# A decoder block's residual gate: summed on TensorE, or along rows on VectorE

## The chip, the cores and the metric

One NeuronCore of a Trainium2 chip runs one program. The metric is the device time of one execution in microseconds (us), the median of several runs. The engines are TensorE (PE, with its weight loads PEld), VectorE (DVE), ScalarE (ACT), GpSimd (POOL) and SyncE (SP), which here only issues DMAs.

## The reference, cut to what matters

The block has 1024 positions, a width of 1024 and one layer. A conditioning vector `c` gives three vectors through one weight matrix; shift and scale act on the normed input, and the gate on the output of the block.

```python
mod = jax.nn.silu(c) @ w_ada + b_ada
shift, scale, gate = jnp.split(mod, 3, axis=-1)
h = rms_norm(x, norm_gain) * (1.0 + scale[:, None, :]) + shift[:, None, :]
proj = h @ w_in                      # q, k, v, z_a, u, z_b, m_a, m_b
p_a = (attn * jax.nn.silu(z_a)) @ w_branch_a       # stick-breaking attention
p_b = (pooled * jax.nn.silu(z_b)) @ w_branch_b     # causal pooling
merged = jax.nn.sigmoid(m_a) * p_a + jax.nn.sigmoid(m_b) * p_b
x = x + gate[:, None, :] * (merged @ w_out)        # then a last rms_norm
```

## The kernel before

Every large product is made of three products of split float32 operands (a high part and a low part), with the contraction in eight row blocks of 128 and the output in tiles of 128 x 512, so that 24 products fill one PSUM bank. The work runs in stages, one after the other on TensorE:

- The start (lines 197 to 530): the input `x` is loaded, its rows are squared and scaled (ScalarE, GpSimd, VectorE), it is turned on TensorE, and shift and scale are applied. Line 201 takes the sigmoid of `c`, held as 128 x 8 (tile `csig`), and line 203 makes its silu (`csilu`). A second copy of the silu, as a row spread over all 128 partitions (`scb`), is made in `spread()`, lines 216 to 223: two products copy the row into PSUM (`crow`), two Sigmoids (line 222) and two multiplies (line 223) follow. Shift and scale are sums along rows: in `modulation()` line 273 multiplies a weight tile that has the output channels on partitions by `scb`, and the instruction's accumulator gives the sum (`mj` is the product that nobody reads, `acc` the sum). From line 376 to 521 each engine keeps the order in which the program is written.
- The value projections and the pooling differences (lines 558 to 595), then the gate branch `wzb` (lines 600 to 614), whose result times the pooled differences is `gb`, split into high and low by lines 610 and 611.
- The second branch product `pb` (lines 617 to 631), eight column tiles of two halves, `gb` times `w_branch_b`, written to DRAM as `pb_d`. In the same loop one row block of the gate's weights is loaded per turn (line 621, 512 KB) and VectorE adds it, times the silu of the block's 128 channels, to `gacc` (lines 623 and 625). `gacc` then holds 128 partial sums for each of 1024 channels. After the loop, lines 633 to 637 sum over the partitions on TensorE with a matrix of ones, and VectorE adds the bias, which line 616 had spread over the partitions by a DMA; line 638 writes one row to DRAM (`g_d`).
- The attention stage (lines 642 to 914), with the projections `p` of keys, queries and gates between the attention's own products. TensorE's order is written out there.
- The last stage (lines 917 to 1000): line 927 reads `g_d` back, spread over the partitions, and line 922 multiplies the output weights by it; then the first branch product `pa` and the output product `o`.

Outside the stretches whose order is written out, a scheduler that simulates the program orders each engine's instructions when the kernel is built. All DMAs of the gate are issued on SP's queue.

Of the kernel before, what the change touches and what calls it, by code (L numbers as in the profile page):

```python
# [9 lines left out]
F32 = mybir.dt.float32  # L10
F32R = mybir.dt.float32r
AF = mybir.ActivationFunctionType
ALU = mybir.AluOpType
PSUM = bass.MemoryType.PSUM

P = 128
D = 1024
S = 1024
KB = D // P
# [35 lines left out]
def block_kernel(ctx, tc, a, out):  # L55
    nc = tc.nc
    v, act, gp = nc.vector, nc.scalar, nc.gpsimd

    def pool(name, **kw):
        return tc.tile_pool(name=name, bufs=1, reuse_waits="tile", **kw)  # L60

    const = ctx.enter_context(pool("const"))
# [5 lines left out]
    def bank(tag, name):  # L68
        return psp.tile([P, 512], F32, tag=tag, bufs=BANKS[tag], name=name)
# [3 lines left out]
    g_d = dram.tile([1, D], F32, name="g_d")  # L73
# [8 lines left out]
    ones = const.tile([P, P], F32, name="ones")  # L82
    gp.memset(ones, 1.0)
    mhalf = const.tile([P, 8], F32, name="mhalf")
    gp.memset(mhalf, -0.5)
    vecs = const.tile([P, 40], F32, name="vecs")
    nc.sync.dma_start(vecs, a["vecs"])
    c_v, gain_v, psc_v = vecs[:, 0:8], vecs[:, 8:16], vecs[:, 16:24]
    bada_v = vecs[:, 24:40]


    pinned = [False]
# [1 line left out]
    def order(op):  # L94
        def issue(*args, **kw):
            ins = op(*args, **kw)  # L96
            if pinned[0]:
                tc.keep_in_program_order(ins)
        return issue

    mm = order(nc.tensor.matmul)
# [20 lines left out]
    def load_w(src, name, hi_eng, lo_eng):  # L122
        raw = wts.tile([P, KB, P], F32, tag="raw", bufs=2, name=name + "_raw")
        nc.sync.dma_start(raw.rearrange("p k c -> p (k c)"), src)
        return split(raw, [P, KB, P], wts, "whl", 2, hi_eng, lo_eng, name)
# [9 lines left out]
    def make_lo(pl, n, tag=None):  # L135

        for _ in range(n):
            i = next(early_lo)
            if tag:
                raw, hi = (pl.tile([P, D], t_, tag=tag, bufs=5, name=f"l{i}_{n_}") for n_, t_ in (("raw", F32), ("hi", F32R)))  # L140
            else:
                raw = pl.tile([P, D], F32, tag="lraw", bufs=3, name=f"l{i}_raw")
                hi = pl.tile([P, D], F32R, tag="lhi", bufs=1, name=f"l{i}_hi")
            nc.sync.dma_start(raw, a["w_in"][tiles[i]])
            act.copy(hi, raw)
            v.tensor_sub(raw.bitcast(F32R), raw, hi.bitcast(F32))
            nc.sync.dma_start(wl_d[i], raw)
# [11 lines left out]
    def mm3(ps, whl, mhl, kbs, mov, first=True, last=True):  # L159
        (wh, wl), (mh, ml) = whl, mhl  # L160
        n = len(kbs)
        for i, kb in enumerate(kbs):
            for j, (w, m) in enumerate(((wh, mh), (wh, ml), (wl, mh))):
                mm(
                    ps, w[:, kb], mov(m, kb),
                    start=first and i == 0 and j == 0, stop=last and i == n - 1 and j == 2,
                )
# [4 lines left out]
    def hmov(sh):  # L172
        return lambda m, kb: m[:, kb, sh * 512:sh * 512 + 512]

    def project(ct, name, use, he, le):
        whl = load_w(a["w_in"][ct], name, he, le)
        for sh in range(2):
            ps = bank("pj", f"{name}_{sh}")
            mm3(ps, whl, (h_hi, h_lo), range(KB), hmov(sh))
            use(sh, ps)  # L180
# [16 lines left out]
    early = ExitStack()  # L197
    first = early.enter_context(pool("first", side="right"))
    with pool("init") as init:
        sig = const.tile([P, 8], F32, name="csig")  # L200
        act.activation(sig, c_v, AF.Sigmoid)
        sc = const.tile([P, 8], F32, name="csilu")
        v.tensor_mul(sc, c_v, sig)

        affb = const.tile([P, 8], F32, name="affb")
        v.scalar_tensor_tensor(affb, bada_v[:, 8:16], 1.0, gain_v, ALU.add, ALU.mult)
# [103 lines left out]
        wg, maps, halves = {}, {}, {}  # L310
# [112 lines left out]
        sl = slice(0, 512)  # L423
# [100 lines left out]
        for i in range(NA, KB):  # L524
            ps = bank("pj", f"u{i}_0")
# [12 lines left out]
    def make_d(j):  # L538
        win = WINDOWS[j // 2]
        u = dif.tile([P, S + 16], F32, tag="u", bufs=2, name=f"u{j}")  # L540
        v.memset(u[:, S:], 0.0)
        nc.sync.dma_start(u[:, :S], u_d[j])
        cur, n, step = u, S + 16, 1
        while step < win:
            nxt = dif.tile([P, S + 16], F32, tag="win", bufs=2, name=f"win{j}_{step}")
            n -= step
            v.tensor_add(nxt[:, :n], cur[:, :n], cur[:, step:step + n])
            cur, step = nxt, 2 * step
        t0 = S - win + 1
        d = dif.tile([P, S], F32, tag="d", bufs=5, name=f"d{j}")  # L550
        v.scalar_tensor_tensor(d[:, :t0], cur[:, :t0], 1.0 / win, u[:, :t0], ALU.mult, ALU.subtract)
        tl = dif.tile([P, 16], F32, tag="tl", bufs=2, name=f"tl{j}")
        v.tensor_mul(tl[:, :win - 1], cur[:, t0:S], invn[:, 16 - win + 1:])
        v.tensor_sub(d[:, t0:], tl[:, :win - 1], u[:, t0:S])
        dhls[j] = d


    with pool("vp") as vp:
# [6 lines left out]
        for i in reversed(range(KB)):  # L565
            ps = bank("pj", f"u{i}_1")
# [5 lines left out]
        dif = diffs.enter_context(pool("dif", side="right"))  # L572
        for hf in range(2):
            if hf == 0:
                wv.append([load_wv(1, k2) for k2 in range(4)])
            for sb in range(8):
                ss = slice(sb * P, (sb + 1) * P)
                ps = bank("pj", f"v{sb}_{hf}")
# [19 lines left out]
    with pool("pb") as pb:  # L598
        gb = pb.tile([P, 2, KB, S], F32R, name="gb")
        for j in range(KB):  # L600
            if j not in dhls:
                make_d(j)
            zs = [pb.tile([P, 512], F32, tag="zs", bufs=3, name=f"zs{j}_{sh}") for sh in range(2)]

            def silu(sh, ps):
                z, sl = zs[sh], slice(sh * 512, sh * 512 + 512)
                act.activation(z, ps, AF.Sigmoid)
                v.tensor_mul(z, ps, z)
                v.scalar_tensor_tensor(z, dhls[j][:, sl], psc_v[:, j:j + 1], z, ALU.mult, ALU.mult)
                act.copy(gb[:, 0, j, sl], z)  # L610
                v.tensor_sub(gb[:, 1, j, sl], z, gb[:, 0, j, sl].bitcast(F32))

            project(CZB + j, f"wzb{j}", silu, act, v)
            del dhls[j]
        gacc, bg = (dif.tile([P, S + 16], F32, tag="u", bufs=2, name=n)[:, :D] for n in ("gacc", "bg"))
        nc.sync.dma_start(bg, a["b_gate"].broadcast_to([P, D]))
        for j in range(KB):
            sm = [pb.tile([P, 512], F32, tag="zs", bufs=3, name=f"sm{j}_{sh}") for sh in range(2)]
            whl = load_w(a["w_branch_b"][j], f"wb{j}", v, gp)
            wg = wts.tile([P, D], F32, tag="raw", bufs=2, name=f"wg{j}")  # L620
            nc.sync.dma_start(wg, a["w_gate"][j * P:(j + 1) * P, :])
            if j == 0:
                v.tensor_scalar_mul(gacc, wg, sc[:, 0:1])
            else:
                v.scalar_tensor_tensor(gacc, wg, sc[:, j:j + 1], gacc, ALU.mult, ALU.add)
            for sh in range(2):
                ps = bank("pj", f"pb{j}_{sh}")
                mm3(ps, whl, (gb[:, 0], gb[:, 1]), range(KB), hmov(sh))
                act.copy(sm[sh], ps)
                nc.sync.dma_start(pb_d[j][:, sh * 512:sh * 512 + 512], sm[sh])  # L630
            make_lo(dif, LO_PB[j], "d")

        for hf in range(2):
            sl = slice(hf * 512, hf * 512 + 512)
            ps = bank("z", f"gate{hf}")
            mm(ps, ones, gacc[:, sl], start=True, stop=True)
            v.tensor_add(bg[:, sl], ps, bg[:, sl])
        nc.sync.dma_start(g_d, bg[0:1, :])
    diffs.close()


# [275 lines left out]
    with pool("fin") as fin:  # L917
# [8 lines left out]
        bg = fin.tile([P, D], F32, name="bg")  # L926
# [5 lines left out]
        for sh in range(2):  # L932
            sl = slice(sh * 512, sh * 512 + 512)
            ms = []
            for j in range(KB):
# [8 lines left out]
                ps = bank("pj", f"pa{sh}_{j}")  # L944
                n = 0
# [12 lines left out]
            for i in range(4):  # L958
# [8 lines left out]
                for c_, cl in enumerate(pieces):  # L967
                    w_ = cl.stop - cl.start
                    ps = bank(("z", "tr")[c_ % 2], f"o{sb}_{c_}")[:, :w_]
                    n = 0  # L970
# [81 lines left out]
```

## Time and profile before

| | us |
|---|---|
| median of 3 runs (1220.42 to 1220.68) | 1220.5 |
| the profiled execution | 1220.86 |
| its span, first to last instruction | 1219.1 |
| TensorE busy in it | 1207.6 (99%) |
| VectorE, ScalarE, GpSimd busy | 789.0, 561.7, 204.6 |

A line of the trace's timeline has the start, the duration, the engine, the line of the kernel, the operation and what it writes and reads, with the idle time ahead of it and what ended that idle time in brackets. Neighbours of the same form are merged, and "x8" counts them. The chain is the work that ended last, followed back from the last instruction. A table by stretches has the length, then for each engine its busy time, the granted TensorE clock as a share of full speed, the DMA share and GB/s.

### The profile page before, as it was taken

The page shows a single profiled execution, that of the slowest core. Times are in us where ns is not written, and L with a number is a line of the kernel's source. Part 1 is how long each engine was busy: PE and PEld are TensorE (multiplying, and loading weights), DVE is VectorE, ACT ScalarE, POOL GpSimd, SP SyncE. Part 2 cuts the span into 40 slices and gives each one's busy share as a digit, 9 for nine tenths or more (in the row PEclk, how much of TensorE's full clock was granted, in tenths as well). Part 3 has the DMA queues.
Part 4 walks back from the last instruction along what each step waited for, and adds up shares of the span by engine and source line. Part 5 has one row for each costly group of instructions (what it writes and reads, how often), then busy time and mean ns, then how long its engine had stood idle before and what let it go on. Part 6 is the DMA issues. An engine that isn't in the chain of part 4 may idle for free.

```text
span 1219.1 us, 16079 instructions
## 1 busy us (share of the span) xinstructions
PE 1207.6 (99%) x5780; PEld 1003.9 (82%) x5780; DVE 789.0 (65%) x1066; ACT 561.7 (46%) x1047; POOL 204.6 (17%) x365
## 2 busy tenths in 40 slices
PE   8999999999999999999999999999999999999997
PEld 7888888888888888888888888888888888888886
DVE  6735494567511388787868778787786763795643
ACT  5555232234301365655656656665655653232211
POOL 1010000000222343222213223221312210000001
PEclk9999999999999999999999999999999999999999
DMA  9638999226843411223424124242233235985612
GB/s 356 232 121 290 325 364 348 87 87 222 311 145 117 138 52 58 90 92 100 130 96 129 57 96 126 96 130 77 84 109 104 95 110 192 336 278 172 212 66 86
DMA packets 72802, 192.43 MB, mean 158 GB/s; under 512 B 7698, under 2 KB 21138, under 8 KB 70804
## 3 DMA queue, kind: packets, MB, share of 16 engines
q1 hardware_dynamic: 61956, 172.35, 40.9%
q10 hardware_dynamic: 10768, 19.08, 4.8%
q8 instruction: 45, 0.74, 0.2%
q14 instruction: 33, 0.27, 0.1%
HBM read 136.86 MB, written 50.34 MB: 154 GB/s over the span
## 4 chain that ended last, share of the span: by engine, by line
PE 94%; DVE 3%; issue 1%; ACT 1%; POOL 0%; POOLq 0%; ACTq 0%; DVEq 0%
PE p L96 34%; PE v L96 7%; PE pb L96 7%; PE wzb L96 7%; PE pa L96 7%; PE o L96 6%; PE z L96 5%; PE av L96 5%; PE wt L96 5%; PE u L96 5%; PE ua L96 3%; PE wm L96 2%; DVE be L96 1%; DVE om L782 1%; DVE kl L96 1%
## 5 line engine op out<-in xcount | busy, mean ns | idle before, releaser
L96 PE MATMUL p<-hT,w 128*128 128x512 f32 x1920 | 534.7, 399 | 0.2 <-DVE kl L96 0.2
L96 PEld LDWEIGHTS p<-hT,w 128*128 128x128 f32 x1920 | 341.4, 188 | 56.6 <-DVE kl L96 0.6
L782 DVE TENSOR_TENSOR_SCAN om<-om 128x512 f32<-128x512 f32 (+7 forms) x128 | 175.8, 1373 | 50.4 <-ACT om L775 25.2
L775 ACT ACTIVATE om<-z 128x512 f32<-128x512 f32 (+2 forms) x192 | 94.5, 492 | 105.3 <-PE z L96 78.4
L802 DVE TENSOR_TENSOR wt<-wt,wt 128x512 fp32r<-128x512 f32 (+1 forms) x160 | 100.7, 629 | 59.8 <-ACT wt L801 58.2
L780 POOL TENSOR_SCALAR_AFFINE_SELECT om<-om 128x128 f32<-128x128 f32 x128 | 68.2, 533 | 333.9 <-ACT om L775 309.9
L801 ACT CAST wt<-wt 128x512 fp32r<-128x512 f32 (+1 forms) x160 | 87.3, 546 | 64.9 <-PE wt L96 63.0
L96 DVE TENSOR_TENSOR be<-be,om 128x511 f32<-128x511 f32 (+7 forms) x128 | 101.3, 799 | 0.7
L96 PE MATMUL av<-wt,vv 128*128 128x512 f32 x320 | 94.1, 375 | 0.0
L776 ACT ACTIVATE be<-z 128x512 f32<-128x512 f32 (+2 forms) x192 | 93.6, 488 | 0.0
L96 PEld LDWEIGHTS wt<-ident,be 128*128 128x128 f32 x576 | 72.3, 140 | 24.2 <-DVE wt L802 2.6
L96 PE MATMUL wt<-ident,be 128*128 128x128 f32 x576 | 89.0, 272 | 1.6 <-DVE wt L802 1.6
L96 PE MATMUL pa<-ga,wa 128*128 128x512 f32 x384 | 89.6, 389 | 0.1
L96 PE MATMUL o<-wo,mhl 128*128 128x512 f32 (+1 forms) x408 | 89.6, 377 | 0.0
L96 PE MATMUL v<-wv,hT 128*128 128x512 f32 x384 | 87.2, 389 | 0.0
L96 PE MATMUL pb<-gb,wb 128*128 128x512 f32 x384 | 87.2, 389 | 0.0
L96 PE MATMUL wzb<-hT,wzb 128*128 128x512 f32 x384 | 87.2, 389 | 0.0
L96 PEld LDWEIGHTS o<-wo,mhl 128*128 128x128 f32 x408 | 73.5, 188 | 14.1
L96 PEld LDWEIGHTS pa<-ga,wa 128*128 128x128 f32 x384 | 72.0, 188 | 15.4 <-DVE wa L111 0.5
L96 PEld LDWEIGHTS v<-wv,hT 128*128 128x128 f32 x384 | 72.1, 188 | 15.0
L96 PEld LDWEIGHTS wzb<-hT,wzb 128*128 128x128 f32 x384 | 72.1, 188 | 15.0
L96 PEld LDWEIGHTS pb<-gb,wb 128*128 128x128 f32 x384 | 72.1, 188 | 15.0
(126 smaller groups left out, 1427.7 us busy)
## 6 DMA issues: line engine op xcount, KB each, us to landing
w_raw<-in_w_in SPq DMA_DIRECT2D x40, 512.0 KB, 4.3
l_raw<-in_w_in SPq DMA_DIRECT2D x32, 512.0 KB, 5.6
wl_d<-l_raw SPq DMA_DIRECT2D x32, 512.0 KB, 4.5
w<-wl_d SPq DMA_DIRECT2D x32, 512.0 KB, 3.7
v_d<-vo SPq DMA_DIRECT2D x16, 512.0 KB, 5.1
vv<-v_d SPq DMA_DIRECT2D x8, 1024.0 KB, 5.8
wa_raw<-in_w_branch_a SPq DMA_DIRECT2D x16, 512.0 KB, 5.3
wa<-in_w_mod SPq DMA_DIRECT2D x7, 1024.0 KB, 7.1
```

Of the source, the lines that this page charges most:

```text
L96: ins = op(*args, **kw)
L775: act.activation(om[:, b0:b0 + n], zp[:, :n], AF.Sigmoid, scale=-0.125)
L776: act.activation(be[:, b0:b0 + n], zp[:, :n], AF.Sigmoid, scale=0.125)
L780: gp.affine_select(out=tl[:, :P], in_=tl[:, :P], pattern=[[1, P]], compare_op=ALU.is_gt, fill=fill, base=0, channel_multiplier=-1)
L782: v.tensor_tensor_scan(om[:, :W], om[:, :W], om[:, :W], 1.0, ALU.mult, ALU.min)
L801: act.copy(wt[:, 0, :off], pt[:, :off])
L802: v.tensor_sub(wt[:, 1, :off], pt[:, :off], wt[:, 0, :off].bitcast(F32))
```

## The change

The gate is summed the way shift and scale are. Its weights are handed over transposed, with the output channels on partitions, in eight tiles of 128 channels. The row of `c` is spread over the partitions by a DMA, its silu is made there (one Sigmoid on ScalarE, one multiply on VectorE), and eight VectorE instructions multiply a weight tile by it and sum along the row into one column of a 128 x 8 tile. The bias is a 128 x 8 tile, and one store writes the 1024 values of 4 bytes to `g_d` in channel order. The 128 x 8 silu at the start goes, and with it 8 columns of the tile `vecs`. The two tiles of the pooling differences' buffers that held `gacc` and the spread bias hold the spread silu and the unread product.

```diff
-    c_v, gain_v, psc_v = vecs[:, 0:8], vecs[:, 8:16], vecs[:, 16:24]
-    bada_v = vecs[:, 24:40]
+    gain_v, psc_v = vecs[:, 0:8], vecs[:, 8:16]
+    bada_v = vecs[:, 16:32]
@@ -197,10 +197,6 @@
-        sig = const.tile([P, 8], F32, name="csig")
-        act.activation(sig, c_v, AF.Sigmoid)
-        sc = const.tile([P, 8], F32, name="csilu")
-        v.tensor_mul(sc, c_v, sig)
@@ -612,17 +608,20 @@
-        gacc, bg = (dif.tile([P, S + 16], F32, tag="u", bufs=2, name=n)[:, :D] for n in ("gacc", "bg"))
-        nc.sync.dma_start(bg, a["b_gate"].broadcast_to([P, D]))
+
+        sg, gjunk = (dif.tile([P, S + 16], F32, tag="u", bufs=2, name=n)[:, :D] for n in ("sg", "gjunk"))
+        nc.sync.dma_start(sg, a["c_row"].broadcast_to([P, D]))
+        act.activation(gjunk, sg, AF.Sigmoid)
+        v.tensor_mul(sg, sg, gjunk)
+        gate = pb.tile([P, KB], F32, name="gate")
+        bias = pb.tile([P, KB], F32, name="gbias")
+        nc.sync.dma_start(bias, a["b_gate"])
         for j in range(KB):
...
-            nc.sync.dma_start(wg, a["w_gate"][j * P:(j + 1) * P, :])
-            if j == 0:
-                v.tensor_scalar_mul(gacc, wg, sc[:, 0:1])
-            else:
-                v.scalar_tensor_tensor(gacc, wg, sc[:, j:j + 1], gacc, ALU.mult, ALU.add)
+            nc.sync.dma_start(wg, a["w_gate"][j])
+            v.scalar_tensor_tensor(gjunk, wg, 1.0, sg, ALU.mult, ALU.mult, accum_out=gate[:, j:j + 1])
...
-        for hf in range(2):
-            sl = slice(hf * 512, hf * 512 + 512)
-            ps = bank("z", f"gate{hf}")
-            mm(ps, ones, gacc[:, sl], start=True, stop=True)
-            v.tensor_add(bg[:, sl], ps, bg[:, sl])
-        nc.sync.dma_start(g_d, bg[0:1, :])
+        v.tensor_add(gate, gate, bias)
+        nc.sync.dma_start(g_d[0].rearrange("(k p) -> p k", p=P), gate)
```

## Rows read from the trace of the kernel before

**Rows 1.** The page: the span, and the chain that ended last, by engine.

```profile
span 1219.1 us, 16079 instructions
...
PE 94%; DVE 3%; issue 1%; ACT 1%; POOL 0%; POOLq 0%; ACTq 0%; DVEq 0%
```

**Rows 2.** The chain in order of time (start, us, what), around the gate's products.

```profile
306.17 87.05 PE pb L96 x384
393.22 1.72 PE gate L96 x4
394.93 21.79 PE p L96 x96
```

**Rows 3.** ScalarE's timeline, the first 15 us.

```profile
0.80 1.28 ACT L201 ACT_TABLE_LOAD   x1 [0.80 <-PEq L1044]
2.53 0.21 ACT L201 ACTIVATE csig<-vecs 128x8 f32<-128x8 f32 x1 [0.45 <-DMA vecs<-in_vecs]
8.67 0.59 ACT L96 CAST wg<-wm 128x512 fp32r<-128x512 f32 x1 [5.93 <-PE wm L96]
10.39 0.59 ACT L96 CAST wg<-wm 128x512 fp32r<-128x512 f32 x1 [1.14 <-PE wm L96]
10.88 1.06 ACT L96 ACTIVATE junk<-x 128x1025 f32<-128x1025 f32 x1
...
11.93 1.07 ACT L96 ACTIVATE sigb<-crow 128x512 f32<-128x512 f32 x2
14.23 0.59 ACT L96 CAST wg<-wm 128x512 fp32r<-128x512 f32 x1 [1.23 <-PE wm L96]
```

**Rows 4.** VectorE's timeline, 12 to 18 us.

```profile
12.55 1.29 DVE L96 TENSOR_TENSOR scb<-crow,sigb 128x512 f32<-128x512 f32 x2 [0.84 <-ACT sigb L96]
...
14.85 0.69 DVE L96 TENSOR_TENSOR wg<-wm,wg 128x512 fp32r<-128x512 f32 x1 [0.35 <-ACT wg L96]
15.45 1.22 DVE L96 SCALAR_TENSOR_TENSOR mj<-wa,scb 128x1024 f32<-128x1024 f32 x1
16.60 0.08 DVE L96 DVE_READ_ACCUMULATOR mj<-wa,scb 128x1 f32 x1
...
17.11 0.75 DVE L96 TENSOR_SCALAR x<-x,st 128x1024 f32<-128x1024 f32 x1 [0.24 <-POOL st L251]
```

**Rows 5.** Two stretches: PE, PEld, DVE, ACT, POOL busy; clock; DMA.

```profile
23.00:28.00 5.00, 3.51 (x20) 2.52 (x19) 4.93 (x10) 3.89 (x8) 0.00 (x0) 1.00 1.01 390
28.00:70.00 42.00, 42.00 (x231) 36.21 (x230) 29.59 (x44) 26.16 (x48) 4.66 (x8) 1.00 0.62 232
```

**Rows 6.** The chain in order of time, at the start.

```profile
23.18 1.15 DVE mj L96 x2
```

**Rows 7.** The gate's tiles: count, ns min/median/max, first and last start, forms.

```profile
L96 PE MATMUL gate<-gacc,ones x4: 592/593/593, 393.1 to 394.3; 128*128 128x512 f32 x4
...
L625 DVE SCALAR_TENSOR_TENSOR gacc<-wg,csilu,gacc x7: 1277/1283/1286, 305.4 to 367.4; 128x1024 f32<-128x1024 f32 x7
...
L623 DVE TENSOR_SCALAR gacc<-wg,csilu x1: 758/758/758, 293.3 to 293.3; 128x1024 f32<-128x1024 f32 x1
```

**Rows 8.** SP's timeline: DMA issues around the gate's store and its reader.

```profile
386.44 0.33 SPq L124 DMA_DIRECT2D w_raw<-in_w_in  x1
...
395.69 0.24 SPq L638 DMA_DIRECT2D g_d<-bg  x1
396.01 0.81 SPq L685 DMA_DIRECT2D vv<-v_d  x2
...
1031.19 0.42 SPq L927 DMA_DIRECT2D bg<-g_d  x1
```

**Rows 9.** VectorE's timeline, the end of the gated tiles.

```profile
309.92 2.44 DVE L609 SCALAR_TENSOR_TENSOR zs<-d,vecs,zs 128x512 f32<-128x512 f32 x1
...
313.42 0.68 DVE L611 TENSOR_TENSOR gb<-zs,gb 128x512 fp32r<-128x512 f32 x1
```

**Rows 10.** A stretch after the last product, columns as in rows 5.

```profile
1214.00:1216.00 2.00, 0.00 (x0) 0.00 (x0) 0.83 (x2) 0.61 (x1) 0.66 (x1) 0.85 0.00 0
```

More of the change, by code (lines that the diff above doesn't have):

```diff
@@ L85, in block_kernel @@
     gp.memset(mhalf, -0.5)
-    vecs = const.tile([P, 40], F32, name="vecs")
+    vecs = const.tile([P, 32], F32, name="vecs")
     nc.sync.dma_start(vecs, a["vecs"])
-    c_v, gain_v, psc_v = vecs[:, 0:8], vecs[:, 8:16], vecs[:, 16:24]
-    bada_v = vecs[:, 24:40]
+    gain_v, psc_v = vecs[:, 0:8], vecs[:, 8:16]
+    bada_v = vecs[:, 16:32]
     pinned = [False]
@@ L1028 @@
         "vecs": np.ascontiguousarray(np.concatenate(
-            [cols(np.asarray(c)[0]), cols(np.asarray(norm_gain)[0]), cols(np.asarray(pool_scale)[0]), b_mod], axis=1)),
+            [cols(np.asarray(norm_gain)[0]), cols(np.asarray(pool_scale)[0]), b_mod], axis=1)),
         "c_row": np.ascontiguousarray(np.asarray(c)[0][None]),
-        "b_gate": np.ascontiguousarray(b[2 * D:][None]),
+        "b_gate": np.ascontiguousarray(cols(b[2 * D:])),
         "final_gain": np.ascontiguousarray(np.asarray(final_gain)[None]),
         "w_mod": np.ascontiguousarray(w_mod).reshape(KB, P, 2 * D),
-        "w_gate": np.ascontiguousarray(wm[:, 2 * D:]),
+        "w_gate": np.ascontiguousarray(wm[:, 2 * D:].T).reshape(KB, P, D),
         "w_in": col_tiles(np.asarray(w_in)[0]),
```

## The prediction

> **What bounds the kernel now.** I read the page first: its span, and the chain that ended last by engine. TensorE carries 94% of that chain [rows 1], so an edit on another engine is worth nothing unless TensorE waits for it, and an edit on TensorE is worth its full time wherever nothing else is late. The second view is that chain in order of time around the place of the change: the eight column tiles of the second branch product, then the gate's products, then the first projection of the attention stage, end to end, all TensorE [rows 2]. The third is the start, on ScalarE and VectorE, since the change also takes two small instructions away there, and the start is the one place before the attention stage where TensorE waits for a VectorE chain [rows 3 to 6].
>
> **The gate's product on TensorE.** The two calls of line 636 are four products of some 592 ns each that overlap [rows 7]; on the chain they hold 1.72 us between the last branch product and the first projection [rows 2]. After the change nothing stands between those two. The branch products run at 87.05 us / 384 = 0.227 us each without a wait, the projections at 21.79 / 96 = 0.227 us, so there is no slower neighbour to give the time back to. What could be late next is the weight tile of the first projections, but its load was issued at 386.44 [rows 8], before the gate's products, and the chain shows no wait behind them. I take the whole 1.72 us off: **-1.72**. The two additions of line 637 go too; they came after the products, and nothing but the store of line 638 waited for them, so they are worth nothing.
>
> **The sums on VectorE.** Removed: one multiply of 0.76 us, seven accumulations of 1.28 us, and the two additions of 128x512, some 0.68 us each like one of that size in the stage [rows 9], 11.1 us. Added: eight products with a sum along the row, for which the start has the same form on the same size, 1.22 us and 0.08 us to read the sum [rows 4], 8 x 1.30 = 10.4 us; one product of 128x1024 with the sigmoid, 1.22 us by the same row; one addition of 128x8, some 0.2 us. In all 11.8 us, 0.7 more. ScalarE gets one Sigmoid of 128x1024, some 1.06 us by the Square of that width [rows 3]. All of it lies beside the branch products. The tightest point there is the low half of the last gated tile: VectorE writes it at 313.42 to 314.10 [rows 9], and TensorE, which starts the branch products at 306.17 [rows 2], takes its last row block in the second half tile after 24 + 21 + 1 products, at 306.17 + 46 x 0.227 = 316.6. The margin is 2.5 us, and ahead of that point the change adds 0.5 us (the first of the eight) and, if the scheduler puts them so late, 1.22 us for the product with the sigmoid. Cost 0, and at most some 2 us if another order of VectorE's queue eats the margin; one instruction of 128x512 there took 2.44 us where another took 0.68 [rows 9], which is how it could.
>
> **The DMAs.** The eight weight loads keep their size and queue. The broadcast of 512 KB into the tile of line 616 stays, with another row as source; the bias becomes a small load of 128x8. The gate leaves as 1024 elements of 4 bytes where one row of 4 KB left before; the trace has no such store. Bounds: the row store took SP's queue 0.24 us, and the reader comes 635 us later; right behind it on that queue stand two loads of value tiles at 396.01 and, at 386.44 ahead of it, the projections' weights [rows 8]. I take 0, and 1 us as the upper end, if the small elements hold up a weight load behind them.
>
> **The start.** Lines 200 to 203 go. The sigmoid there is 0.21 us and hidden, but it is the instruction in front of which the run's only activation table load stands: 1.28 us at 0.80, while ScalarE has nothing to do until 8.67 [rows 3]. Something must load a table for what comes next on ScalarE, and that is the Square at 10.88 and then the two Sigmoids at 11.93, which feed the row that VectorE needs at 12.55 [rows 3, 4]. The casts before them are not activations. So the load moves from idle time into a busy queue. How many loads there are, no row shows. I take two: the load of before was placed for the instruction right behind it; the first activation is now a Square, and a load that is placed for a Square need not bring a table with Sigmoid, so a second one stands ahead of the Sigmoids.
>
> The sum for two loads: 2 x 1.28 = 2.57 us, and 0.10 us for each load, because the Square started 0.10 before the cast ahead of it was over [rows 3], an overlap which I expect to lose at each load. The first VectorE product at 12.55 comes 2.77 us later. On VectorE it then meets two gaps, 0.35 us before 14.85 and 0.24 us before 17.11 [rows 4], and hardly another: from 23 to 28 us VectorE is busy 4.93 of 5.00 us [rows 5]. ScalarE's own queue recovers in its waits for TensorE (1.23 us before 14.23 [rows 3]), so VectorE sets it: the modulation product at 23.18, which is on the chain [rows 6], comes 2.77 - 0.59 = 2.18 us later. TensorE waits 1.49 of the 5.00 us up to 28 and nothing in the 42 us behind it [rows 5], so all of it is passed on. Bounds: 0, if the load lands in the idle time; 3.1 us, if each load is followed by the 0.45 us that passed between the load of before and the sigmoid (there it was the input's DMA that ended it [rows 3], so I stay near the lower figure). I take **+2.2**.
>
> The Trainium skill (ScalarE: Activation LUTs, What ACT_TABLE_LOAD costs) speaks against this part of the change more strongly: it gives the load 1283 ns, as the trace does, and some 1380 ns of drain with each switch to another set, 2.66 us in all. By that the two loads would be 5.3 us and the time, as an estimate from that page, 1223.7 us; the trace has an activation 0.45 us after the end of its load, which speaks against the drain.
>
> **The sum.** -1.72 + 2.2 = +0.5 us. Against the profiled execution, 1220.86 us (a span of 1219.1 and 1.8 around it), that is 1221.3; the median of the runs is 0.36 lower, 1220.5, and so is the forecast: **1221.0 us**.
>
> **The rivals.** *One load in the queue.* If one table serves Square and Sigmoid, one load stands before the Square: 1.28 + 0.10 less the 0.59 of gaps is +0.8, and the time 1220.5 - 1.72 + 0.8 = 1219.6. For it speaks that one load serves every ScalarE instruction of the run before; against it, that it was chosen for a Sigmoid. The Trainium skill (ScalarE activation tables: per-element evaluation and per-set limits, Table sets in the compiler and the runtime) says that the compiler's back end takes for a block the set that serves the longest run of activations; by that rule it would be this rival. The single load of the trace agrees with that rule and with the other.
>
> *No load on the path.* If the load is set at the head of the program, as the one of before was in effect, the start is unchanged and only the gain is left: 1218.8. For it: the queue is empty until 8.67. Against it: the load of before carries the line of its activation.
>
> *The change doesn't do what it says* would be a gate product that stays; the diff removes both calls, so I give it nothing.
>
> *The clock, the slower side.* Place: 22.7 to 27 us, where TensorE already waits 1.49 us and would wait some 3.7. Price: the granted clock was 1.00 throughout there [rows 5], 2.4 GHz; at the end, with TensorE idle from 1214 to 1216, it is 0.85 on average [rows 10], so it has begun to fall to 1.2 GHz there. If it falls in the longer gap too, the 3.5 us of products of this stretch [rows 5] run at half speed and take some 2 to 3 us more: 1221.0 + 2.5 = 1223.5. It decides as soon as the granted clock of the stretch falls at all; against it, the wait is broken by the transposes and by products, while at the end the engine had stopped for good.
>
> *VectorE's order in the pooling stage* (above): up to 2 us of TensorE waiting near 311 to 317 us, 1221 to 1223.
>
> **How the numbers follow.** Two loads 0.58 (1220.9 to 1221.8), one load 0.12 (1219.6), no load 0.12 (1218.8), clock 0.10 (1223.5), VectorE's order 0.08. 0.2% is 2.4 us, about what a measurement here tells from no change: faster is below 1218.1, slower above 1222.9. Of these cases only the lower edge of the third is faster, 0.04; the clock and a third of the last case are slower, 0.13; 0.83 is the same. The range takes in the first three cases and most of the last: 1218.7 to 1222.7.
>
> **What would show it.** The rows of after should have no gate product, with the first projection following the last branch product within 0.25 us; one or two table loads on ScalarE's timeline between 10.5 and 14.5 us, and a first product of line 223 on VectorE near 15.3 us; TensorE running without a wait from some 30 us rather than 28. Wrong would be: a table load at 0.8 us again, a start as before with 1.7 us gained; a granted clock under 1.00 before 30 us; TensorE waiting between 306 and 318 us; or a wait of the attention stage for the store of the gate.

## The result and the profile after

The changed kernel takes 1225.74 us (median, 1225.58 to 1226.96) against 1220.79 us in the runs beside it: 1.0041 times the time before, with a 95% interval of 1.0029 to 1.0054. The forecast was 1221.0 us with a range up to 1222.7, so the change is slower than the range allowed. "Slower" had been given a chance of 0.13, for a falling clock and for VectorE's order, neither of which came. The profiled execution has a span of 1224.1 us, 5.0 more than before.

The chain in order of time, of the kernel after (start, us, what); rows 2 are its counterpart.

```profile
28.20 2.80 PE ua L96 x12
...
100.74 34.00 PE u L96 x144
134.74 87.06 PE v L96 x384
221.80 87.04 PE wzb L96 x384
308.84 87.04 PE pb L96 x384
395.88 21.76 PE p L96 x96
...
1040.05 22.41 PE pa L96 x96
...
1177.69 28.84 PE o L96 x127
```

The same view of the kernel before, at the places that rows 2 do not hold:

```profile
28.02 2.76 PE ua L96 x12
...
99.10 32.95 PE u L96 x144
132.05 87.07 PE v L96 x384
219.13 87.04 PE wzb L96 x384
...
1038.00 21.76 PE pa L96 x96
...
1172.77 28.80 PE o L96 x127
```

The product of `gate` is gone, and `p` follows `pb` at once, as forecast. But with the same work 144 products of `u` take 34.00 us instead of 32.95 (0.236 us each instead of 0.229), and 96 of `pa` take 22.41 instead of 21.76 (0.233 instead of 0.227), while `v`, `wzb`, `pb`, the first `p` and the long run of `o` keep their pace. From the starts in the two chains, and the ends of the spans, one gets where the 5.0 us came from:

| stretch | before, us | after, us | difference |
|---|---|---|---|
| to the products of `ua` at 28 us | 28.02 | 28.20 | +0.18 |
| from there (`ua`, `u`, `v`, `wzb`) to `pb` | 278.15 | 280.64 | +2.49 |
| `pb` and the gate, to the first `p` | 88.76 | 87.04 | -1.72 |
| attention stage, to `pa` | 643.07 | 644.17 | +1.10 |
| last stage, to the end | 181.10 | 184.05 | +2.95 |

The 1.10 us of the attention stage lie in the attention's own products `z`: in the stretch from 390 to 1040 us TensorE is busy with them for 98.54 us before and 99.60 us after.

TensorE's idle time explains little of it: its longest waits of the run after, by line and releaser, are these (us in total, times, longest), and at 34 to 70 us, as in rows 5, it is busy throughout.

```profile
PE idle L96 <- POOL x L227: 1.6, 1, 1.6
PE wt L96 <- DVE wt L797: 1.4, 3, 0.7
PE ua L96 <- ACT hT L96: 1.1, 1, 1.1
PE ua L96 <- DVE wg L96: 1.0, 1, 1.0
PE wm L96 <- DMA praw<-in_pool_w: 0.8, 1, 0.8
```

The wait for `praw` is not in the list of before, and that for `wg` is 0.6 us longer; both fall into the first 28 us, which differ by 0.18 us in all. The second was, before the change:

```profile
PE ua L96 <- DVE wg L96: 0.4, 1, 0.4
```

The start, first on ScalarE and then on VectorE, against rows 3 and 4:

```profile
0.79 1.28 ACT L96 ACT_TABLE_LOAD   x1 [0.79 <-PEq L1040]
...
9.98 0.58 ACT L96 CAST wg<-wm 128x512 fp32r<-128x512 f32 x1 [1.14 <-PE wm L96]
10.46 1.06 ACT L96 ACTIVATE junk<-x 128x1025 f32<-128x1025 f32 x1
...
11.63 1.28 ACT L96 ACT_TABLE_LOAD   x1
12.93 1.08 ACT L96 ACTIVATE sigb<-crow 128x512 f32<-128x512 f32 x2
```

```profile
13.56 1.29 DVE L96 TENSOR_TENSOR scb<-crow,sigb 128x512 f32<-128x512 f32 x2 [2.26 <-ACT sigb L96]
...
15.42 0.68 DVE L96 TENSOR_TENSOR wg<-wm,wg 128x512 fp32r<-128x512 f32 x1
...
17.37 0.74 DVE L96 TENSOR_SCALAR x<-x,st 128x1024 f32<-128x1024 f32 x1
```

There are two table loads, but the first, ahead of the Square, was issued at 0.79, in the idle time; the second stands ahead of the two Sigmoids. The Squares behind the Sigmoids need no third load, and before the change the one load ahead of `csig` served all: what is loaded for the Sigmoid serves the Square too, while behind the load for the Square the Sigmoid got one of its own. VectorE's first product of the row comes at 13.56 instead of 12.55, and both of its gaps of rows 4 are gone.

The gate's own instructions, by tile (count, ns min/median/max, first and last start, form):

```profile
L624 DVE SCALAR_TENSOR_TENSOR gjunk<-wg,sg x8: 1216/1226/1228, 295.7 to 370.1; 128x1024 f32<-128x1024 f32 x8
...
L633 SPq DMA_DIRECT2D g_d<-gate x1: 386/386/386, 371.8 to 371.8; - x1
```

### The profile page after: what moved, and what is told of

Same layout as the page of the kernel before. It is cut to its first block, busy times and chain, and to the rows that moved or that the text cites. A ratio compares the mean times of both kernels' runs of the same rounds, so it can differ in the third digit from the quotient of the medians.

```text
span 1224.1 us, 16080 instructions
## 1 busy us (share of the span) xinstructions
PE 1211.5 (99%) x5776; PEld 1002.6 (82%) x5776; DVE 788.9 (64%) x1073; ACT 563.4 (46%) x1048; POOL 204.8 (17%) x365
## 4 chain that ended last, share of the span: by engine, by line
PE 94%; DVE 3%; ACT 1%; issue 1%; DMA 0%; POOL 0%; SPq 0%; POOLq 0%; DVEq 0%; ACTq 0%
PE p L96 35%; PE pa L96 7%; PE v L96 7%; PE pb L96 7%; PE wzb L96 7%; PE o L96 6%; PE z L96 5%; PE av L96 5%; PE wt L96 5%; PE u L96 5%; PE ua L96 3%; PE wm L96 1%; DVE be L96 1%; PE xt L96 1%; DVE kl L96 0%
## 5 line engine op out<-in xcount | busy, mean ns | idle before, releaser
L96 PE MATMUL pa<-ga,wa 128*128 128x512 f32 x384 | 92.2, 396 | 0.0
```

## The experiments

The two theories after the result were these. A: the change makes the block of constants 96 bytes per partition smaller (8 columns of `vecs` and the two tiles `csig` and `csilu`, 32 bytes each). Pools without `side="right"` are laid out upward behind the constants, the others downward from the right end, so the left tiles moved by 96 bytes and the right ones did not. The constants add up to 1376 bytes per partition before, which leaves 96 when divided by 128, and to 1280 after, which leaves 0; the large tiles on the left start behind them. That the large tiles on the right start at 96 is the reading of the memory maps, which no view shown here holds; the shift of the left side against the right one follows from the edits alone. The slow products are those whose stationary and moving operands come from different sides: `ua` and `u` take their weights from `wg` on the right and `hT` on the left, `pa` its weights from the left and `ga` from the right. `z` does not fit these words: its operands `kh`, `kl` and `q` all lie on the right. B: the new order of the queues, or the new DMAs, disturb TensorE.

| run | left side, right side, by 128 | us | before, beside it | ratio to before, 95% |
|---|---|---|---|---|
| change | 0, 96 | 1225.74 | 1220.79 | 1.0041 (1.0029 to 1.0054) |
| e1, change, left padded by 96 | 96, 96 | 1219.53 | 1220.85 | 0.9989 (0.9980 to 0.9998) |
| e2, change, right padded by 96 | 0, 0 | 1218.71 | 1220.85 | 0.9985 (0.9976 to 0.9995) |
| e3, before, padded by 32 | 0, 96 | 1226.95 | 1220.85 | 1.0050 (1.0035 to 1.0065) |
| e4, before, padded by 64 | 32, 96 | 1224.51 | 1220.85 | 1.0029 (1.0017 to 1.0041) |
| e8, before, padded by 96 | 64, 96 | 1227.26 | 1221.95 | 1.0047 (1.0033 to 1.0061) |
| e9, before, 32 within the left side | see below | 1235.98 | 1220.61 | 1.0123 (1.0106 to 1.0140) |

The kernel before has 96, 96.

### e1: the changed kernel with the 96 bytes put back

```diff
     vecs = const.tile([P, 32], F32, name="vecs")
+    pad = const.tile([P, 24], F32, name="pad")
+    gp.memset(pad, 0.0)
```

> The changed kernel with 96 unused bytes per partition put back among the constants, so that every tile on the left side of SBUF has the address that it had before. Theory A (addresses: TensorE's products slow down where the stationary and the moving operand come from opposite sides of SBUF, because the 96 bytes that the change frees shifted the left side against the right one): the products of u take 0.229 us each again instead of 0.236, those of pa 0.227 instead of 0.233; the start to the first value product, the attention stage and the last stage regain 2.5, 1.1 and 2.9 us; the time is 1225.7 - 6.5 = 1219.2 us. Theory B (the new order of the other engines' queues, or the new DMAs, disturbs TensorE): nothing of this moves, 1225.7 us.

Measured: 1219.53 us. The chain, in order of time:

```profile
99.44 32.95 PE u L98 x144
...
393.63 21.76 PE p L98 x96
1036.65 21.76 PE pa L98 x96
```

Both paces are those of before. The stage from `p` to `pa` takes 643.02 us and the last stage 181.15, also as before, and `z` is back at 98.56 us. Everything else of the change, its queues and its DMAs, is in this kernel, so theory B falls: all that TensorE's products lost is in where the tiles lie.

### e2: the changed kernel, the right side moved as well

```diff
+    edge = ctx.enter_context(pool("edge", side="right"))
...
     vecs = const.tile([P, 32], F32, name="vecs")
+    pad = edge.tile([P, 24], F32, name="pad")
+    gp.memset(pad, 0.0)
```

> The changed kernel as it is on the left side, with 96 unused bytes at the right end of SBUF, so that the right side moves down by as much as the left side did. Theory A as a matter of the two sides' distance: paces as before the change, 1219.2 us. Theory A as a matter of the left side's own address: as changed, 1225.7 us. Theory B: 1225.7 us.

Measured: 1218.71 us. In the chain:

```profile
98.96 32.95 PE u L99 x144
...
1035.76 21.76 PE pa L99 x96
```

The left side lies where the change put it, and the paces are the good ones. So neither address of the left side is bad by itself; its distance to the right side counts.

### e3: the kernel before with 32 more bytes

```diff
     vecs = const.tile([P, 40], F32, name="vecs")
+    pad = const.tile([P, 8], F32, name="pad")
+    gp.memset(pad, 0.0)
```

> The kernel before with 32 more unused bytes among the constants, which gives the left side the same remainder by 128 as in the changed kernel (0, the right side 96) and leaves all else. Theory A: the slow paces without the change, 1220.8 + 6.5 = 1227.3 us. Theory B: 1220.8 us.

Measured: 1226.95 us. The chain has the slow paces beside the gate's product:

```profile
100.19 33.86 PE u L98 x144
...
395.18 1.72 PE gate L98 x4
...
1041.58 22.40 PE pa L98 x96
```

An unused tile of 32 bytes costs this kernel 6.1 us, more than the whole change does. The 6.5 us that I had summed from the stages was 0.4 too high.

### e4 and e8: other distances

The same edit with 16 and with 24 columns instead of 8.

> The kernel before with 64 more unused bytes among the constants: the left side's remainder is 32 by 128, as the right side's is by 64. If what counts is the remainder by 64, 1220.8 us; if it is by 128, some slow pace, up to 1227.3 us. Theory B: 1220.8 us.

Measured: 1224.51 us. `u` is between the two paces, `pa` as slow as after the change:

```profile
99.36 33.23 PE u L98 x144
...
1039.38 22.40 PE pa L98 x96
```

So a shift of 64 bytes is not free either: a common remainder by 64 is not enough.

> The kernel before with 96 more unused bytes among the constants: the left side's remainder by 128 is 64, the right side's 96, a distance of 32 to the other side than in the changed kernel. If the distance by 128 counts whichever side is ahead, the paces of the changed kernel and 1226.9 us; if the sign counts, or only some remainders are good, another time between 1220.8 and 1227.

Measured: 1227.26 us, with `u` at 33.86 us for 144 and `pa` at 22.48 for 96. By the remainders this is a distance of 32 bytes with the other side ahead, and the paces are those of e3. No run has a smaller distance, and none shifts one side by a full 128 bytes, so that the pace returns there is the reading of the remainders and not a measurement.

### e5, e6 and e7: the table load

To the kernel of e1 (e6) and to that of e2 (e7) one early Sigmoid is added; e5 is e1 once more, as their neighbour.

```diff
     with pool("init") as init:
+        act.activation(pad[:, 0:8], mhalf, AF.Sigmoid)
```

> The changed kernel with the left side's addresses of before, once more, as the neighbour of the next run on the same chip: 1219.5 us as the first time.

> The same with one Sigmoid of 128x8 on a constant tile as ScalarE's first instruction, where the kernel before had its own. Theory: the one load that stands on the path (1.28 us ahead of the two Sigmoids of the row) goes back into the idle time; VectorE's first product of the row comes some 1.3 us earlier, VectorE meets its two gaps of 0.35 and 0.24 us again, and the time is 0.7 us lower, 1218.8 us; from before to here only the gate's products are then left, 1220.8 - 1.7 = 1219.1. Rival (the load is hidden behind VectorE's other work): 1219.5 us, the same.

> The changed kernel with the right side moved by 96 bytes, as in the second run, and the early Sigmoid: both costs of the change taken out in the other way. 1218.0 to 1218.8 us; if the load is hidden, 1218.7 as the second run.

Measured beside each other: 1220.13 us (0.9990, 0.9981 to 1.0000), 1219.52 us (0.9986, 0.9977 to 0.9995) and 1219.51 us (0.9981, 0.9972 to 0.9990). The kernel before took 1221.95 us beside them (1220.23 to 1224.35), and all three lie above what was expected, by 0.6 to 1.5 us. The order is the expected one, but the intervals overlap, so the times alone do not settle half a microsecond. The trace of e7 does; ScalarE, VectorE, and the chain:

```profile
2.09 0.21 ACT L203 ACTIVATE pad<-mhalf 128x8 f32<-128x8 f32 x1
...
9.99 0.59 ACT L99 CAST wg<-wm 128x512 fp32r<-128x512 f32 x1 [1.14 <-PE wm L99]
...
11.53 1.07 ACT L99 ACTIVATE sigb<-crow 128x512 f32<-128x512 f32 x2
```

```profile
14.45 0.69 DVE L99 TENSOR_TENSOR wg<-wm,wg 128x512 fp32r<-128x512 f32 x1 [0.35 <-ACT wg L99]
...
16.72 0.75 DVE L99 TENSOR_SCALAR x<-x,st 128x1024 f32<-128x1024 f32 x1 [0.24 <-POOL st L251]
```

```profile
27.62 2.76 PE ua L99 x12
```

Counted from ScalarE's second cast to the products of `ua`, so that the executions' different first microseconds drop out, before takes 28.02 - 10.39 = 17.63 us, after 28.20 - 9.98 = 18.22, e1 28.34 - 10.13 = 18.21, and e7 27.62 - 9.99 = 17.63. In these traces the load on the path costs 0.59 us, and the early Sigmoid of e7 gives that back. In e6 the stretch takes 28.12 - 10.03 = 18.09 us although its load is gone and both of VectorE's gaps are back. VectorE has a further gap there, ahead of the scaling of the fourth row block, and behind it stands ScalarE's Square of that block, which waited for the input:

```profile
21.80 0.88 DVE L98 TENSOR_SCALAR x<-x,st 128x128 f32<-128x128 f32 x2 [0.43 <-POOL st L250]
```

```profile
19.98 1.06 ACT L98 ACTIVATE junk<-x 128x1025 f32<-128x1025 f32 x1 [0.36 <-DMA x<-in_x]
```

The same wait for the load of `x` stands in e4 (0.39 us) and e8 (0.28 us), which have no load on the path either: their stretches take 28.00 - 9.89 = 18.11 us and 27.74 - 9.72 = 18.02, while e3 and e9, without this wait, take 17.62. So the early Sigmoid is worth 0.59 us where the input is there in time, and 0.1 to 0.2 us where it is late. One profile of each kernel does not tell how often that is. The profile of e6 is one of its longer executions, 1222.16 us, and its attention stage takes 646.03 us, 3 us more than that of e1; this was not pursued.

### e9: 32 bytes within the left side

```diff
     big = ctx.enter_context(pool("big"))
+    edge = ctx.enter_context(pool("edge"))
     wts = ctx.enter_context(pool("wts"))
...
     vecs = const.tile([P, 40], F32, name="vecs")
+    pad = edge.tile([P, 8], F32, name="pad")
+    gp.memset(pad, 0.0)
```

> The kernel before with 32 unused bytes between the resident activations (the tile hT, which later is wo) and everything else on the left side: hT and the whole right side stay at the remainder 96 by 128, the weight tiles, gb, wv and the merged tiles move to 0. Theory A (the distance between the stationary and the moving operand of each product) says product by product which are slow: u (wg from the right with hT) stays at 0.229 us each; pb (weight tiles with gb, both moved) stays at 0.227; v (hT with wv), wzb and p (weight tiles with hT), pa (weight tiles with ga from the right) and o (merged tiles with wo) go to 0.233 to 0.236. These are 384 + 384 + 1920 + 384 + 408 = 3480 products, x 0.0067 to 0.009 = 23 to 31 us: 1244 to 1252 us. A theory in which one side of SBUF as such or the right side's tiles are slow: 1220.8, or u slow.

Measured: 1235.98 us. The chain:

```profile
99.16 32.96 PE u L99 x144
132.12 89.60 PE v L99 x384
221.72 89.59 PE wzb L99 x384
311.31 87.07 PE pb L99 x384
398.38 1.72 PE gate L99 x4
400.10 22.39 PE p L99 x96
...
1048.60 22.40 PE pa L99 x96
...
1187.20 29.65 PE o L99 x127
```

In long runs of like products it is what theory A said: `u` and `pb`, whose operands kept their distance, keep 0.229 and 0.227 us; `v`, `wzb`, `p`, `pa` and `o`, whose operands lie 32 bytes apart, take 0.233 us each. The sum was missed: 15.4 us and not 23 to 31. The attention stage lost 648.50 - 643.07 = 5.4 us where 1920 products of `p` at 0.0067 would be 12.8. The pages of before and of e9 give the busy time of all `p`:

```profile
L96 PE MATMUL p<-hT,w 128*128 128x512 f32 x1920 | 534.7, 399 | 0.2 <-DVE kl L96 0.2
L99 PE MATMUL p<-hT,w 128*128 128x512 f32 x1920 | 539.5, 402 | 0.1
```

So 4.8 of the 5.4 us are in `p`, but at 0.0025 us for each product, where the 96 in one run lose 0.0063. Most `p` stand between transposes, `z` and `av`; why the distance costs them less is open. The transposes `wt` themselves lose nothing: their `ident` stayed while `be` moved, and they are busy 89.0 us before and 88.9 in e9.

## Why the prediction was wrong

- **The gate's product, -1.72.** Right: from the start of `pb` to the first `p` the chain has 1.72 us less.
- **The sums on VectorE, 0.** Right. The Sigmoid (1.07 us, at 259 us) and its product ran beside `wzb`, the eight products of 1.23 us from 295.7 to 371.3 us beside `wzb` and `pb`; from 306 to 318 us TensorE is busy for all 12.00 us. VectorE writes the last low half of `gb` at 317.12 to 317.81, and TensorE takes it at 308.84 + 46 x 0.227 = 319.3, so the margin went from 2.5 to 1.5 us.
- **The DMAs, 0.** Right in cost: the store of 1024 single elements takes 13.4 us from issue to landing, and nobody waits for it.
- **The start, +2.2.** Too large by 1.6. That there would be two loads was right, that both would stand in the queue was not: the first was issued at 0.79, ahead of the casts that wait for TensorE, and the prediction had named a load at 0.8 us as a sign of being wrong. What failed here is the placing of the Square's load behind the cast ahead of it. One load stood on the path, as in the first rival, though it was the Sigmoid's and not the Square's, and it cost 0.59 us where that rival had 0.8. The Trainium skill (ScalarE: Activation LUTs, What ACT_TABLE_LOAD costs) gives 1380 ns of drain for a switch; it is not in the trace: the Sigmoid begins at 12.93, 0.02 us after the load that ended at 12.91. The Trainium skill (ScalarE activation tables: per-element evaluation and per-set limits, Table sets in the compiler and the runtime) says that the compiler's back end places the loads for each block by the longest run. The trace does not agree: this program loads one set for the Square and another for the Sigmoid, though the second serves both. In both places the measurement decides.
- **The term that was missing.** This is the step that made the forecast wrong: it put what the removed tiles do to the addresses at nothing, without a reason. "Lines 200 to 203 go" was costed by the instructions and the load alone, and the 8 columns of `vecs` not at all. Those lines and columns also hold 96 bytes in front of every tile of the left side. Taking the 96 bytes back (e1) takes 1225.74 to 1219.53, 6.2 us: -1.72 + 0.59 + 6.2 = +5.1, measured +4.95. The miss was only 4.7 us by luck, since the 1.6 us too many at the start hid a part of the 6.2. The clock, which I had as the slower side, stayed at 1.00 from 23 to 28 us, where I had set its fall, and at 1.00 from 70 to 140 us, where the slow `u` run; the weight loads of `u` keep their median of 188 ns in both kernels.

What in TensorE makes the distance cost time, whether the loading of the next weights meets the reading of the present moving operand or something else, is open; no run separates it. That `z`, with all its operands on one side, slows down as well speaks against the distance between a product's own two operands being the whole account. The lowest ratio of the study is that of e7, the change with its two side effects taken out: 0.9981 of the time before (0.9972 to 0.9990), but its interval overlaps those of e1, e2 and e6.

## What to carry to other kernels

A change that only removes a small tile moves every tile allocated behind it on the same side; where a kernel's pools grow from both ends of SBUF, compare the start addresses of the two operands of the large products before and after, and keep their difference as it was. That any multiple of 128 bytes would do is likely by the remainders, but was not measured. An uneven slowdown shows in the chain as a pace: divide each run of like products by its count in both kernels before looking for waits. When the first instruction of ScalarE is removed, look at what it loaded.

## What was not expected of the hardware

TensorE's pace in long runs of products depends on where the two operands lie relative to each other. With the distances of the kernel before, equal remainders by 128, a product of 128x128 by 128x512 takes 0.227 us (`wzb`) to 0.229 (`u`); with 32 bytes more or less by the remainders 0.233 to 0.236; with 64 bytes 0.231 (`u`) and 0.233 (`pa`). The granted clock is 1.00 in the slow runs, no wait stands in them, and VectorE is as busy after as before (788.9 and 789.0 us). Transposes of 128x128 do not show it (e9). An unused tile of 32 bytes made this kernel 0.5% slower in one place (e3) and 1.2% in another (e9).
